# A summed weight factor made by an accumulating load instead of by VectorE, in all twelve blocks of seven products of a decoder trunk

## The chip, the cores and the metric

The kernel runs on one core of a Trainium2 chip. The metric is the device time of one execution in microseconds. The kernel before takes 912.77 us, the median of three runs from 911.77 to 912.87 us.

## What is computed

A trunk of two layers over 256 tokens of width 1024 in float32. Each layer is a gated feed-forward, a mixer with three groups of heads, and a second gated feed-forward, each between two RMS norms:

```python
def _swiglu(h, wg, wu, wd):
    return (jax.nn.silu(h @ wg) * (h @ wu)) @ wd

for l in range(DEPTH):                                       # DEPTH = 2
    f = _swiglu(_rmsnorm(h, ff1_norm_pre[l]), ff1_w_gate[l], ff1_w_up[l], ff1_w_down[l])
    h = h + 0.5 * _rmsnorm(f, ff1_norm_post[l])
    m = _hybrid_mixer(_rmsnorm(h, mix_norm_pre[l]), ...)     # SSD, pooling, attention; not touched here
    h = h + _rmsnorm(m, mix_norm_post[l])
    f = _swiglu(_rmsnorm(h, ff2_norm_pre[l]), ff2_w_gate[l], ff2_w_up[l], ff2_w_down[l])
    h = h + 0.5 * _rmsnorm(f, ff2_norm_post[l])
```

The gate and up weights are 1024 x 2816, the down weights 2816 x 1024. There are four feed-forwards, so four times the stage that the change touches.

## The kernel before

**Units and splits.** All weights come through one object, `Weights` (L50 to L158). A *unit* is a piece of 1 MB, 128 partitions x 2048 float32, loaded by SP into one of five `raw` buffers (`load`, L85). A *job* splits a unit for the matmuls: ScalarE writes a rounded copy `hi` (L114) and VectorE the rest, `lo = raw - hi` (L115), in two halves of 1024 columns (a "`hi` half", a "`lo` half"), into one of five pairs of buffers. A matmul product then is three passes: x_hi w_hi, x_hi w_lo, x_lo w_hi. A job may first make a sum of two units: VectorE adds them into the first one's buffer, at L113 half by half, or at L133 all at once ahead of the split. A job may end with an accumulating load: POOL issues a DMA that adds a unit from memory onto a buffer (`then`, L119). A job's `free` list names the `raw` buffers that it gives back.

**Feed-forward.** The 2816 hidden columns are eleven groups of 256. Groups 0 and 1 (FIRST) and the single ones 4, 7 and 10 (PAIRS) are plain products. Groups 2-3, 5-6 and 8-9 (QUADS, starting at 2, 5 and 8) are the *blocks of seven*: gate and up for 512 columns would be eight products of a 128 x 512 half row block of x by a 512 x 512 weight quarter, and Winograd's form of Strassen's scheme makes them from seven. I call the blocks of a feed-forward the *opening*, the *middle* and the *closing* one: three in each of four feed-forwards, twelve in all.

The right factors of the seven products are made from four weight quarters, g1, u1, g2 and u2 (gate and up, each with the upper and the lower half of the rows). With their left factors, in the order of the products in `ffn_quad`: g1 with X11; the first sum T1 = g1 + u1 with S1; the second sum T2 = T1 + u2 with S2; T3 = u1 + u2 with S3; g2 with X12; the *fourth factor* T4 = T2 + g2 with X22; and u2 with S4. T1, T2 and T4 are all made in the buffer of g1, by VectorE. T3 is made in the buffer of u1 by an accumulating load of u2, issued by POOL behind the sum T1. In the code the order of loads and splits is the order of the calls of `W.unit` and `W.job` in `plan_ffn` (L422).

**The products and their sums.** In `ffn_quad` (L563) the product of T2 is joined to that of g1 (L586, L587). The product of T3 lies in a bank `pd`: VectorE adds a term to it (L598) and reads it (L599), and then the product of T4 accumulates on top of it in the same bank. ScalarE takes silu of the result (L619), VectorE multiplies (L620, L630), and the hidden columns go to the transposes (L533, or a DMA) and the down products (`mm_rows`, L412).

**What sets the order.** Each engine works through its queue in order. The queues are laid down by a scheduler at build time: it takes the code's order, `issue_after` and `keep_in_program_order`, and moves what it holds to be ready. What it has laid down does not change on the chip. Inside the kernel `pump` (L136) hands out loads and splits when buffers are free. In the closing block `sum_next` (L133) makes the sum of T4 right behind the product of T1, ahead of its split; in the opening block it makes that of T2.

Of the kernel before, what the change touches and what calls it, by code (L numbers as in the profile page):

```python
# [15 lines left out]
ALU = mybir.AluOpType  # L16
AX = mybir.AxisListType

P = 128
# [3 lines left out]
DEPTH = 2  # L23
# [7 lines left out]
UNIT = 2048  # L31
# [4 lines left out]

FIRST, QUADS, PAIRS = (0, 1), (2, 5, 8), (4, 7, 10)

# [11 lines left out]
class Weights:  # L50
# [75 lines left out]
    def sum_next(self):  # L126
        u, sum_of, _, pieces, _ = self.jobs[self.split]
        assert sum_of and self.ready()
        x, op, y = sum_of
        step = self.units[u][1] // pieces  # L130
        for c in range(0, self.units[u][1], step):
            s = slice(c, c + step)
            self.nc.vector.tensor_tensor(self.raw[u][:, s], self.raw[x][:, s], self.raw[y][:, s], op=op)  # L133
        self.summed = self.split
# [27 lines left out]
def hybrid_trunk_kernel(ctx: ExitStack, tc: tile.TileContext, a, out: bass.AP):  # L162
# [259 lines left out]
    def plan_ffn(l, n):  # L422


        p = {}

        def down(i):
            p["d", i] = W.plan(a[f"ff{n}_d"][l, i])

        def pair(i):  # L430
            for k in "gu":
                p[k, i] = W.plan(a[f"ff{n}_{k}"][l, PAIRS.index(i)])

        for i in range(2):
            for k in range(2):
                p["f", i, k] = W.plan(a[f"ff{n}_f"][l, 2 * i + k], pieces=4)
        before = list(FIRST)
        for i in range(2, NU):
            if i in PAIRS:
                pair(i)  # L440
                for b in before:
                    down(b)
                before = [i]
            elif i in QUADS:
                src = a[f"ff{n}_q"][l, QUADS.index(i)]
# [7 lines left out]
                if not late:  # L453
# [108 lines left out]

    def ffn_quad(i, p, left, turn, downs, by_dma, two, take=None):  # L563

# [29 lines left out]
        if not late:  # L594
            downs[0]()
# [4 lines left out]
        if late:  # L600
            pump_behind(m)
        elif swap:
            pump_behind(m, SPLIT_BUFS, 1)
        else:
            W.pump()
        product(pa, left["X12"], p["g2", i], False)
        h0 = buf()
# [34 lines left out]
    def ffn(l, n, p, gain, turned, left, next_left, before_next, last, later=None):  # L642

        acc = [None, None]
        hT = {}
        by_dma, start = True, later is not None

        def two(i):
            return i == QUADS[-1] or i == QUADS[1] or i == QUADS[0] and not start

# [24 lines left out]
        for i in range(2, NU):  # L675
            if i not in QUADS + PAIRS:
                continue
            order = (1, 0) if i in QUADS or i == PAIRS[0] and two(QUADS[0]) else (0, 1)
            if hf:
# [3 lines left out]
            def turn():  # L683
# [7 lines left out]
                by_tile(turn_tile, 1)  # L691
                take()
# [16 lines left out]
            else:  # L709
                hf = ffn_quad(i, p, left, turn, [lambda b=b: both(b) for b in before], by_dma,  # L710
                              two(i))
                before = [i, i + 1]
# [532 lines left out]
def _layout(inp):  # L1245
# [18 lines left out]

    def quads(g, u):


        q = []
        for i in QUADS:
            for h in range(2):  # L1270
                for w in (g, u):
                    x = w[:, h * 512 : (h + 1) * 512, i * 256 : i * 256 + 512]
                    q.append(x.reshape(DEPTH, 4, P, 512).transpose(0, 2, 1, 3).reshape(DEPTH, P, UNIT))
        return np.stack(q, axis=1).reshape(DEPTH, len(QUADS), 4, P, UNIT)

    for n in (1, 2):
        g, u = f[f"ff{n}_w_gate"], f[f"ff{n}_w_up"]
        d[f"ff{n}_f"] = np.concatenate([half(g[:, :, :512]), half(u[:, :, :512])], axis=1)
        d[f"ff{n}_g"] = cols(g)[:, PAIRS]
        d[f"ff{n}_u"] = cols(u)[:, PAIRS]  # L1280
        d[f"ff{n}_q"] = quads(g, u)
        d[f"ff{n}_d"] = rows(f[f"ff{n}_w_down"])
# [39 lines left out]
```

## Time and profile before

| | |
|---|---|
| median of three runs | 912.77 us (911.77 to 912.87) |
| profiled execution: its own time, from its first to its last instruction (the span) | 910.8 us |
| granted TensorE clock | 0.999 |
| TensorE matmul, weight load | 99%, 84% busy |
| VectorE, ScalarE, GpSimd | 88%, 73%, 3% busy |
| moved by DMA | 198.63 MB, 12.58 MB of it by POOL's queue |

For the profiled execution no other time is recorded than the span; the runs' times also hold what lies around it. In the rows of the profile, PE is TensorE's matmuls, PEld its weight loads, DVE VectorE, ACT ScalarE, POOL GpSimd, SP the engine that issues most DMAs. A row of the timeline gives start and duration in us, the engine, the line, the operation, output and inputs, and how many instructions it joins; brackets give the idle time ahead of it and what ended it. Rows overlap somewhat: two VectorE instructions of 1.21 us take 2.35 us together.

### The profile page before, as it was taken

What the parts mean: (1) busy time and instruction counts of PE and PEld (TensorE: products, weight loads), DVE (VectorE), ACT (ScalarE), POOL (GpSimd) and SP (SyncE); (2) the same over time, 40 slices, a digit from 0 to 9 for tenths busy, and PEclk for the clock granted to TensorE, in tenths of its full rate; (3) what the DMA queues carried; (4) which work ended last, traced back from release to release, by engine and by line L of the source; (5) the groups of instructions that cost most, each with busy time, mean ns of one, the idle gap of its engine ahead of it and who ended that gap; (6) DMA issues with size and microseconds to landing.
All of it is one profiled execution on the core that took longest, in us unless ns stands there. A gap on an engine that the chain in (4) does not pass through costs nothing.

```text
span 910.8 us, 12262 instructions
## 1 busy us (share of the span) xinstructions
PE 901.0 (99%) x4556; PEld 760.6 (84%) x4556; DVE 801.6 (88%) x1068; ACT 665.9 (73%) x1045; POOL 29.8 (3%) x49
## 2 busy tenths in 40 slices
PE   8999999999999999999999999999999999999997
PEld 5888888889988888888888888888998888888885
DVE  6999988789878999988899999988989699999983
ACT  7776776778858777776878768767797668768772
POOL 0000000000001000000000000000000110000000
PEclk9999999999999999999999999999999999999999
DMA  9677977765355587768755968695824256978641
GB/s 360 181 274 227 384 188 282 251 214 204 78 195 208 128 314 205 289 162 288 244 187 149 339 196 299 173 305 200 298 109 162 93 173 180 323 214 298 177 124 47
DMA packets 60880, 198.63 MB, mean 218 GB/s; under 512 B 35858, under 2 KB 36370, under 8 KB 38804
## 3 DMA queue, kind: packets, MB, share of 16 engines
q1 hardware_dynamic: 58948, 185.13, 58.5%
q0 software_dynamic: 1728, 12.58, 7.3%
q8 instruction: 36, 0.59, 0.2%
q14 instruction: 24, 0.20, 0.1%
q10 hardware_dynamic: 144, 0.13, 0.0%
HBM read 188.65 MB, written 1.05 MB: 208 GB/s over the span
## 4 chain that ended last, share of the span: by engine, by line
PE 92%; DVE 5%; issue 2%; DMA 1%; ACT 0%; POOLq 0%; SPq 0%; POOL 0%; DVEq 0%
PE acc L412 29%; PE wk L559 23%; PE wk L390 13%; PE wk L359 9%; PE wk L350 6%; PE wk L361 5%; DVE lo L115 3%; PE wk L377 1%; PE wk L301 1%; DMA raw<-in_ff_f 1%; PE wk L1084 1%; PE acc L827 0%; DVE raw L113 0%; PE acc L897 0%; PE acc L1032 0%
## 5 line engine op out<-in xcount | busy, mean ns | idle before, releaser
L115 DVE TENSOR_TENSOR lo<-raw,hi 128x1024 fp32r<-128x1024 f32 (+2 forms) x452 | 464.3, 1076 | 37.4 <-ACT hi L114 36.8
L114 ACT ACTIVATE hi<-raw 128x1024 fp32r<-128x1024 f32 (+2 forms) x452 | 398.7, 937 | 72.2 <-DVE raw L113 30.1
L412 PE MATMUL acc<-hi,t 128*128 128x512 f32 x832 | 214.7, 391 | 0.0
L412 PEld LDWEIGHTS acc<-hi,t 128*128 128x128 f32 x832 | 155.0, 188 | 31.4
L412 PE MATMUL acc<-lo,t 128*128 128x512 f32 x416 | 113.4, 390 | 0.0
L559 PE MATMUL wk<-hi,n 128*128 128x512 f32 x384 | 100.5, 390 | 0.0
L390 PE MATMUL wk<-hi,xT 128*128 128x512 f32 x384 | 98.9, 393 | 0.2
L359 PE MATMUL wk<-xT,hi 128*128 128x512 f32 x384 | 95.9, 392 | 0.0
L412 PEld LDWEIGHTS acc<-lo,t 128*128 128x128 f32 x416 | 77.9, 188 | 16.3
L390 PEld LDWEIGHTS wk<-hi,xT 128*128 128x128 f32 x384 | 71.0, 188 | 16.4 <-ACT hi L114 1.6
L559 PEld LDWEIGHTS wk<-hi,n 128*128 128x128 f32 x384 | 71.8, 188 | 14.8
L359 PEld LDWEIGHTS wk<-xT,hi 128*128 128x128 f32 x384 | 69.8, 189 | 13.0
L559 PE MATMUL wk<-hi,xT 128*128 128x512 f32 x288 | 77.6, 390 | 0.1
L113 DVE TENSOR_TENSOR raw<-raw,raw 128x1024 f32<-128x1024 f32 x56 | 67.2, 1215 | 0.0
L559 PEld LDWEIGHTS wk<-hi,xT 128*128 128x128 f32 x288 | 53.8, 188 | 11.3 <-DVE t L599 0.4
L361 PEld LDWEIGHTS wk<-xT,lo 128*128 128x128 f32 x384 | 52.4, 190 | 3.8
L361 PE MATMUL wk<-xT,lo 128*128 128x256 f32 x384 | 53.5, 282 | 0.0
L559 PE MATMUL wk<-lo,n 128*128 128x512 f32 x192 | 52.1, 390 | 0.0
L390 PE MATMUL wk<-lo,xT 128*128 128x512 f32 x192 | 52.0, 391 | 0.0
L510 ACT ACTIVATE t<-t 128x1024 uint16<-128x1024 uint16 x31 | 32.6, 1055 | 24.4 <-DVE t L630 16.2
L390 PEld LDWEIGHTS wk<-lo,xT 128*128 128x128 f32 x192 | 36.0, 188 | 8.3 <-DVE lo L115 0.8
L559 PEld LDWEIGHTS wk<-lo,n 128*128 128x128 f32 x192 | 36.0, 188 | 7.7 <-DVE lo L115 0.2
(184 smaller groups left out, 947.8 us busy)
## 6 DMA issues: line engine op xcount, KB each, us to landing
raw<-in_ff_q SPq DMA_DIRECT2D x48, 1024.0 KB, 6.4
raw<-in_ff_d SPq DMA_DIRECT2D x44, 1024.0 KB, 5.1
raw<-in_ff_f SPq DMA_DIRECT2D x16, 1024.0 KB, 7.1
raw<-in_ff_q POOLq DMA_DIRECT2D x12, 1024.0 KB, 8.0
raw<-in_ff_g SPq DMA_DIRECT2D x12, 1024.0 KB, 4.8
raw<-in_ff_u SPq DMA_DIRECT2D x12, 1024.0 KB, 4.8
raw<-in_w_in SPq DMA_DIRECT2D x10, 1024.0 KB, 5.3
raw<-in_w_kvz SPq DMA_DIRECT2D x8, 1024.0 KB, 6.1
```

The costliest lines, as they stand in the source:

```text
L113: nc.vector.tensor_tensor(raw[:, s], self.raw[x][:, s], self.raw[y][:, s], op=op)
L114: self.act = nc.scalar.activation(hi[:, s], raw[:, s], AF.Copy)
L115: nc.vector.tensor_tensor(lo[:, s], raw[:, s], hi[:, s].bitcast(F32), op=ALU.subtract)
L301: pre_turn.last = nc.tensor.transpose(ps[:, k * P : (k + 1) * P], xn[i][:, k * P : (k + 1) * P], ident)
L350: nc.tensor.matmul(ps, w[:, k, s], y[:, k, :], start=i == 0 and k == 0, stop=i == 2 and k == KD - 1)
L359: nc.tensor.matmul(ps, hi[:, k, s], both[:, :, k, :], start=k == 0, stop=k == KD - 1)
L361: mm_side.end = nc.tensor.matmul(ps[:, S:], lo[:, k, s], xT[0][:, k, :], start=False, stop=k == KD - 1, skip_group_check=True)
L377: nc.tensor.matmul(ps, x[:, k, s], w[:, k, :], start=i == 0 and k == 0, stop=i == 2 and k == KD - 1)
L390: m = nc.tensor.matmul(ps, y[:, k, :], w[:, k, :], start=h == 0 and n == 0, stop=h == 1 and n == len(parts) - 1)
L412: m = nc.tensor.matmul(acc[b], x[:, j, s], w[:, j, b * 512 : (b + 1) * 512], start=first and j == 0 and i == 0, stop=last and j == 1 and i ...
L510: part = send.last = nc.scalar.activation(halves.rearrange("p (a n) -> p a n", a=2), x[:, :].bitcast(U16).rearrange("p (n a) -> p a n", a= ...
L559: nc.tensor.matmul(ps, x[:, k, :], w[:, k, :], start=first and n == 0, stop=n == len(parts) - 1, skip_group_check=not first)
```

## The change

T4 is no longer a sum by VectorE. The job of T2 gets an accumulating load behind it, of g2 onto the buffer of g1, which then holds T2 and so becomes T4. The job of T4 only splits that buffer. g2 is still loaded a second time on its own, for its own product, and its buffer is now given back after its own split and no longer after T4's. The rest of the diff has no effect in this form: `shape` returns the same groups for every feed-forward, `close` is never true (ahead of a block there is always FIRST or a single group), the weights' tensors are named by layer, and `sum_next` returns where there is no sum to make.

```diff
+def shape(l, n):
+    return (2, 5, 8), (4, 7, 10)
+
+def last_sum_loaded(l, n):
+    return True
...
     def sum_next(self):
         u, sum_of, _, pieces, _ = self.jobs[self.split]
-        assert sum_of and self.ready()
+        if not sum_of or not self.ready() or self.summed == self.split:
+            return
...
                 p["T1", i] = W.job(g1, (g1, ALU.add, u1), then=(u1, src[3]))
-                p["T2", i] = W.job(g1, (g1, ALU.add, u2))
+                p["T2", i] = W.job(g1, (g1, ALU.add, u2), then=(g1, src[2]) if loaded else None)
...
                 p["T3", i] = W.job(u1, free=(u1,))
                 g2 = W.unit(src[2])
...
-                p["g2", i] = W.job(g2)
+                p["g2", i] = W.job(g2, free=(g2,) if loaded else ())
...
-                p["T4", i] = W.job(g1, (g1, ALU.add, g2), free=(g1, g2))
+                p["T4", i] = W.job(g1, free=(g1,)) if loaded else W.job(g1, (g1, ALU.add, g2), free=(g1, g2))
...
         if late:
             pump_behind(m, SPLIT_BUFS - 1)
+            W.sum_next()
```

The scheduler lays the queues down anew. TensorE, second feed-forward of layer 0, opening block: the fourth factor (`hi67`, `lo67`) and u2 (`hi68`, `lo68`), before:

```order
L559 MATMUL wk362_3050<-hi68_3151,n366_3070 128x512 x4
L559 MATMUL wk362_3050<-lo68_3152,n366_3070 128x512 x2
L559 MATMUL wk373_3159<-hi67_3111,xT_108 128x512 x4
L559 MATMUL wk373_3159<-lo67_3112,xT_108 128x512 x4
L559 MATMUL wk373_3159<-hi67_3111,xT_108 128x512 x4
L559 MATMUL wk362_3050<-lo68_3152,n366_3070 128x512 x2
L559 MATMUL wk362_3050<-hi68_3151,n367_3071 128x512 x4
```

and now (L575 is the line that was L559):

```order
L575 MATMUL wk373_3155<-hi67_3111,xT_108 128x512 x4
L575 MATMUL wk373_3155<-lo67_3112,xT_108 128x512 x4
L575 MATMUL wk373_3155<-hi67_3111,xT_108 128x512 x4
L575 MATMUL wk362_3048<-hi68_3147,n366_3068 128x512 x4
L575 MATMUL wk362_3048<-lo68_3148,n366_3068 128x512 x4
L575 MATMUL wk362_3048<-hi68_3147,n367_3069 128x512 x4
```

The fourth factor's product has moved ahead of all of u2's; it stood behind six of its matmuls. In the opening blocks of layer 1 it is the same, and in the first feed-forward it now stands behind two, before behind seven.

VectorE in the same place: `lo65` is g2, `lo66` a down unit, `lo69` the next gate unit; L587, L598 and L599 are the sums named above. Before:

```order
L115 TENSOR_TENSOR lo65_3083<-raw55_2843,hi65_3082 128x1024 x2
L115 TENSOR_TENSOR lo66_3089<-raw56_3018,hi66_3088 128x1024 x2
L587 TENSOR_TENSOR wk362_3050<-wk362_3050,t355_3033 128x512
L115 TENSOR_TENSOR lo67_3112<-raw51_2533,hi67_3111 128x1024
L113 TENSOR_TENSOR raw51_2533<-raw51_2533,raw55_2843 128x1024
L115 TENSOR_TENSOR lo68_3152<-raw53_2819,hi68_3151 128x1024 x2
L115 TENSOR_TENSOR lo67_3112<-raw51_2533,hi67_3111 128x1024
L598 TENSOR_TENSOR wk373_3159<-wk373_3159,t355_3033 128x512
L115 TENSOR_TENSOR lo69_3175<-raw57_3080,hi69_3174 128x1024
L599 TENSOR_TENSOR t363_3063<-t363_3063,wk373_3159 128x512
```

and now:

```order
L603 TENSOR_TENSOR wk362_3048<-wk362_3048,t355_3031 128x512
L126 TENSOR_TENSOR lo65_3081<-raw55_2840,hi65_3080 128x1024 x2
L126 TENSOR_TENSOR lo66_3089<-raw56_3016,hi66_3088 128x1024 x2
L126 TENSOR_TENSOR lo67_3112<-raw51_2530,hi67_3111 128x1024 x2
L126 TENSOR_TENSOR lo68_3148<-raw53_2816,hi68_3147 128x1024 x2
L615 TENSOR_TENSOR wk373_3155<-wk373_3155,t355_3031 128x512
L126 TENSOR_TENSOR lo69_3171<-raw57_3078,hi69_3170 128x1024
L616 TENSOR_TENSOR t363_3061<-t363_3061,wk373_3155 128x512
```

The sum (its other half stood ten rows higher) is gone, both halves of the fourth factor stand ahead of u2, and five `lo` halves stand between the first of them and L616, which was L599.

VectorE, same feed-forward, closing block: `lo88` is T3, `lo89` g2, `lo90` u2, `lo91` the fourth factor. Before:

```order
L115 TENSOR_TENSOR lo88_3797<-raw71_3563,hi88_3796 128x1024
L133 TENSOR_TENSOR raw70_3531<-raw70_3531,raw73_3649 128x1024
L115 TENSOR_TENSOR lo89_3829<-raw73_3649,hi89_3828 128x1024 x2
L133 TENSOR_TENSOR raw70_3531<-raw70_3531,raw73_3649 128x1024
L115 TENSOR_TENSOR lo90_3865<-raw72_3586,hi90_3864 128x1024 x2
L586 TENSOR_TENSOR t419_3847<-wk422_3874,t419_3847 128x512
L587 TENSOR_TENSOR wk420_3849<-wk420_3849,t419_3847 128x512
L115 TENSOR_TENSOR lo91_3890<-raw70_3531,hi91_3889 128x1024 x2
L598 TENSOR_TENSOR wk423_3899<-wk423_3899,t419_3847 128x512
L599 TENSOR_TENSOR t421_3862<-t421_3862,wk423_3899 128x512
```

and now:

```order
L126 TENSOR_TENSOR lo88_3793<-raw71_3558,hi88_3792 128x1024
L126 TENSOR_TENSOR lo89_3825<-raw73_3644,hi89_3824 128x1024 x2
L126 TENSOR_TENSOR lo90_3863<-raw72_3581,hi90_3862 128x1024 x2
L602 TENSOR_TENSOR t419_3845<-wk422_3870,t419_3845 128x512
L603 TENSOR_TENSOR wk420_3847<-wk420_3847,t419_3845 128x512
L126 TENSOR_TENSOR lo91_3886<-raw70_3526,hi91_3885 128x1024 x2
L615 TENSOR_TENSOR wk423_3893<-wk423_3893,t419_3845 128x512
L616 TENSOR_TENSOR t421_3860<-t421_3860,wk423_3893 128x512
```

Only the sums have gone; TensorE's queue is the same there. SP's queue holds the same transfers in the same order throughout.

More of the change, by code (lines that the diff above doesn't have):

```diff
@@ L35 @@
 TAIL = 4
-FIRST, QUADS, PAIRS = (0, 1), (2, 5, 8), (4, 7, 10)
+FIRST = (0, 1)
+def shape(l, n):
+    return (2, 5, 8), (4, 7, 10)
+def last_sum_loaded(l, n):
+    return True
 C_ID, C_U, C_SGT, C_NEG, C_CNT, C_CS = 0, 128, 256, 384, 512, 1024
@@ L425, in plan_ffn @@
         p = {}
+        QUADS, PAIRS = shape(l, n)
+        loaded = last_sum_loaded(l, n)
         def down(i):
@@ L431, in pair @@
             for k in "gu":
-                p[k, i] = W.plan(a[f"ff{n}_{k}"][l, PAIRS.index(i)])
+                p[k, i] = W.plan(a[f"ff{l}{n}_{k}"][PAIRS.index(i)])
         for i in range(2):
@@ L444, in plan_ffn @@
             elif i in QUADS:
-                src = a[f"ff{n}_q"][l, QUADS.index(i)]
+                src = a[f"ff{l}{n}_q"][QUADS.index(i)]
                 g1, u1, u2 = (W.unit(src[k]) for k in (0, 1, 3))
@@ L452, in plan_ffn @@
                 late, swap = i == QUADS[-1], i != QUADS[0]
-                if not late:
+                close = before[0] in QUADS
+                if not late and not close:
                     down(before[0])
@@ L456, in plan_ffn @@
                 g2 = W.unit(src[2])
-                p["g2", i] = W.job(g2)
+                if not late and close:
+                    down(before[0])
+                p["g2", i] = W.job(g2, free=(g2,) if loaded else ())
                 for b in before[1:]:
@@ L561, in product, with ffn_quad @@
         W.done(job)
-    def ffn_quad(i, p, left, turn, downs, by_dma, two, take=None):
+    def ffn_quad(i, p, left, turn, downs, by_dma, two, QUADS, close, loaded):
         late, swap = i == QUADS[-1], i != QUADS[0]
@@ L593, in ffn_quad @@
             W.pump()
-        if not late:
+        if not late and not close:
             downs[0]()
@@ L605, in ffn_quad @@
             W.pump()
+        if not late and close:
+            downs[0]()
         product(pa, left["X12"], p["g2", i], False)
@@ L646, in ffn @@
         by_dma, start = True, later is not None
+        QUADS, PAIRS = shape(l, n)
         def two(i):
-            return i == QUADS[-1] or i == QUADS[1] or i == QUADS[0] and not start
+            return i in QUADS and (i != QUADS[0] or not start)
         hf = [ffn_first(0, p, later is not None, turned, by_dma=by_dma)]
@@ L677, in ffn @@
                 continue
-            order = (1, 0) if i in QUADS or i == PAIRS[0] and two(QUADS[0]) else (0, 1)
+            order = (1, 0) if i in QUADS or before[0] == QUADS[0] and two(QUADS[0]) else (0, 1)
             if hf:
@@ L690, in turn @@
                     return
-                by_tile(turn_tile, 1)
+                by_tile(receive if two(before[0]) else turn_tile, 1)
                 take()
@@ L710, in ffn @@
                 hf = ffn_quad(i, p, left, turn, [lambda b=b: both(b) for b in before], by_dma,
-                              two(i))
+                              two(i), QUADS, before[0] in QUADS, last_sum_loaded(l, n))
                 before = [i, i + 1]
@@ L1263, in half, with quads @@
         return x.reshape(DEPTH, 2, 4, P, 512).transpose(0, 1, 3, 2, 4).reshape(DEPTH, 2, P, UNIT)
-    def quads(g, u):
+    def quads(g, u, starts):
         q = []
-        for i in QUADS:
+        for i in starts:
             for h in range(2):
                 for w in (g, u):
-                    x = w[:, h * 512 : (h + 1) * 512, i * 256 : i * 256 + 512]
-                    q.append(x.reshape(DEPTH, 4, P, 512).transpose(0, 2, 1, 3).reshape(DEPTH, P, UNIT))
-        return np.stack(q, axis=1).reshape(DEPTH, len(QUADS), 4, P, UNIT)
+                    x = w[h * 512 : (h + 1) * 512, i * 256 : i * 256 + 512]
+                    q.append(x.reshape(4, P, 512).transpose(1, 0, 2).reshape(P, UNIT))
+        return np.stack(q).reshape(len(starts), 4, P, UNIT)
     for n in (1, 2):
@@ L1278, in _layout @@
         d[f"ff{n}_f"] = np.concatenate([half(g[:, :, :512]), half(u[:, :, :512])], axis=1)
-        d[f"ff{n}_g"] = cols(g)[:, PAIRS]
-        d[f"ff{n}_u"] = cols(u)[:, PAIRS]
-        d[f"ff{n}_q"] = quads(g, u)
+        for l in range(DEPTH):
+            starts, singles = shape(l, n)
+            d[f"ff{l}{n}_g"] = cols(g[l : l + 1])[0, list(singles)]
+            d[f"ff{l}{n}_u"] = cols(u[l : l + 1])[0, list(singles)]
+            d[f"ff{l}{n}_q"] = quads(g[l], u[l], starts)
         d[f"ff{n}_d"] = rows(f[f"ff{n}_w_down"])
```

## The prediction

> **What bounds the kernel now.** I read the engines' shares first, then the chain that ended last, then TensorE's own waits, because an engine can be busy and still be the one that waits. The page of the profile:
>
> ```profile
> span 910.8 us, 12262 instructions
> PE 901.0 (99%) x4556; PEld 760.6 (84%) x4556; DVE 801.6 (88%) x1068; ACT 665.9 (73%) x1045; POOL 29.8 (3%) x49
> PE 92%; DVE 5%; issue 2%; DMA 1%; ACT 0%; POOLq 0%; SPq 0%; POOL 0%; DVEq 0%
> ```
>
> TensorE is busy for all but 9.8 us of the span, and 92% of the chain is its own. A busy TensorE need not be at full pace, so I look at the spacing in the chain in order of time, and at all that TensorE and its weight load waited for (us in total, times, longest):
>
> ```profile
> 78.45 10.91 PE acc L412 x48
> 102.95 10.88 PE wk L559 x48
> ...
> PE acc L225 <- DVE zeros L214: 2.3, 1, 2.3
> PE wk L533 <- DVE t L630: 0.7, 1, 0.7
> PE wk L301 <- DVE n L291: 0.2, 1, 0.2
> ...
> PEld wk L559 <- DVE t L599: 0.4, 1, 0.4
> ```
>
> 48 matmuls take 10.91 us in the one and 10.88 us in the other, 0.227 us each: the pace does not change between a down product (L412) and a product of a block of seven (L559). In the whole program TensorE waits three times for another engine, and of the three only the 0.7 us behind L630 lies in a feed-forward stage; the 0.4 us behind L599 is the weight load's. So VectorE, 88% busy, is hidden everywhere but at one place: the opening block of the first feed-forward. That place, in the chain, then on TensorE, then on VectorE:
>
> ```profile
> 53.79 2.27 DVE raw L113 x2
> 72.23 0.63 PE wk L533 x4
> ...
> 59.91 1.07 PE L559 MATMUL wk<-hi,n 128*128 128x512 f32 x4
> 61.85 1.19 PE L559 MATMUL wk<-hi,xT 128*128 128x512 f32 x4
> 72.23 0.63 PE L533 MATMUL wk<-ident,t 128*128 128x128 f32 x4 [0.67 <-DVE t L630]
> ...
> 53.71 2.35 DVE L113 TENSOR_TENSOR raw<-raw,raw 128x1024 f32<-128x1024 f32 x2
> 61.12 0.68 DVE L599 TENSOR_TENSOR t<-t,wk 128x512 f32<-128x512 f32 x1
> ```
>
> The two L113 rows at 53.71 are the sum of the fourth factor, the very work that goes. They stand on the chain, but the chain only says that VectorE's queue from there on released TensorE at 72.23, 0.67 us late. That 0.67 us, not the 2.27 us, is what their removal can pay.
>
> **What goes.** The fourth factor's sum is two instructions in each of twelve blocks: 16 on L113 and 8 on L133 (in the closing blocks `sum_next` makes it).
>
> ```profile
> L113 DVE TENSOR_TENSOR raw<-raw,raw x56: 1208/1215/1221, 28.9 to 847.1; 128x1024 f32<-128x1024 f32 x56
> L133 DVE TENSOR_TENSOR raw<-raw,raw x16: 1210/1216/1221, 34.7 to 857.9; 128x1024 f32<-128x1024 f32 x16
> ```
>
> 24 x 1.215 = 29.2 us of VectorE. In eleven blocks TensorE never waited behind them, so there they are worth nothing; what hides them is the 0.227 us pace above. In the first block VectorE's queue comes 2.27 us earlier to L630, more than the 0.67 us it was late, so that wait is gone: -0.67. The 0.4 us behind L599 stays. TensorE now reaches the fourth product after two matmuls of the u2 product (59.91 + 2 x 0.227 = 60.36), not after seven (61.85). VectorE, from 53.79 with nothing idle, does five `lo` halves of 1.14 (half of 2.27, as in the row), L598 and L599 (1.3): 53.79 + 5.7 + 1.3 = 60.8. A wait of 0.4 us before, of 0.5 after: 0.1 lost.
>
> **What comes.** Twelve more accumulating loads of 1 MB on POOL's queue, each with a wait for the second sum's split. POOL has only other such loads and the norms' powers behind it, and is busy 3% of the span, so the instruction itself costs nothing. No load of SP is moved past another; g2's buffer no longer waits for the sum, so the load that takes it starts up to 2 us sooner. The price is latency: the fourth factor is now there when the load has landed. The rows of the twelve accumulating loads of before, one landing alone, one behind other loads, and SP's two loads issued ahead of the latter:
>
> ```profile
> L119 POOL DMA_DIRECT2D raw<-in_ff_q x12: 853/868/1035, 31.9 to 842.0; - x12
> DMA to landing us min/median/max: 7.8/8.0/11.3
> ...
> DMA to landing us min/median/max: 7.9/7.9/7.9
> ...
> DMA to landing us min/median/max: 11.2/11.2/11.2
> ...
> 519.70 0.53 SPq L85 DMA_DIRECT2D raw<-in_ff_d  x1
> 520.33 0.39 SPq L85 DMA_DIRECT2D raw<-in_ff_q  x1
> ```
>
> The 7.9 is the one issued at 396.50, with no load of SP about; the 11.2 is that of 523.0. How long may one take before TensorE feels it? In a closing block (second feed-forward of layer 0), on VectorE, ScalarE, TensorE and SP, with the two rows by which I time POOL's start behind VectorE:
>
> ```profile
> 405.57 3.50 DVE L115 TENSOR_TENSOR lo<-raw,hi 128x1024 fp32r<-128x1024 f32 x3 [1.55 <-ACT hi L114]
> 417.19 2.35 DVE L115 TENSOR_TENSOR lo<-raw,hi 128x1024 fp32r<-128x1024 f32 x2
> 420.18 0.69 DVE L599 TENSOR_TENSOR t<-t,wk 128x512 f32<-128x512 f32 x1
> ...
> 413.11 2.00 ACT L114 ACTIVATE hi<-raw 128x1024 fp32r<-128x1024 f32 x2
> ...
> 423.30 1.07 PE L559 MATMUL wk<-hi,xT 128*128 128x512 f32 x4
> ...
> 409.09 0.33 SPq L85 DMA_DIRECT2D raw<-in_ff_g  x1
> ...
> 303.64 1.22 DVE L113 TENSOR_TENSOR raw<-raw,raw 128x1024 f32<-128x1024 f32 x1
> 305.16 0.89 POOL L119 DMA_DIRECT2D raw<-in_ff_q  x1 [11.67 <-DVE raw L113]
> ```
>
> The second sum's split ends with the second of the three `lo` rows at 405.57, at 407.9. POOL starts 0.3 us behind VectorE (304.86 to 305.16). From the landing on: 1.05 us for the first `hi` half on ScalarE (two, overlapping, take 2.00), two `lo` halves (2.3), then L598 and L599, 1.3 from the end of the `lo` at 419.54 to 420.87. L599 reads the bank into which the fourth product accumulates, and it stands on VectorE behind the `lo` halves, so TensorE, due at 423.30, waits for all of it: 4.7 us with 0.05 for the semaphore. The landing may take 423.3 - 407.9 - 0.3 - 4.7 = 10.4 us; I carry 10.3. Past that, each us of landing costs TensorE one us. In the opening blocks of the three later feed-forwards, in a middle block, and in the first of all:
>
> ```profile
> 311.65 2.35 DVE L115 TENSOR_TENSOR lo<-raw,hi 128x1024 fp32r<-128x1024 f32 x2
> ...
> 332.95 1.07 PE L559 MATMUL wk<-hi,n 128*128 128x512 f32 x4
> ...
> 312.90 0.33 SPq L85 DMA_DIRECT2D raw<-in_ff_d  x1
> ...
> 84.96 4.62 DVE L115 TENSOR_TENSOR lo<-raw,hi 128x1024 fp32r<-128x1024 f32 x4
> ...
> 110.95 1.07 PE L559 MATMUL wk<-hi,xT 128*128 128x512 f32 x4
> ...
> 38.15 4.62 DVE L115 TENSOR_TENSOR lo<-raw,hi 128x1024 fp32r<-128x1024 f32 x4
> ```
>
> Opening: the split ends at 314.00, and the fourth product is now due at 332.95, where the u2 product stood. Behind the landing are 1.05, five `lo` halves (5.7), L598 and L599, 8.1 us together: 18.95 - 0.3 - 8.1 = 10.5 us of room. Middle: from 89.6 at the latest to 110.95 are 21.4 us, and 0.3 + 11.3 + 4.7 go in with 5 to spare. First of all: the split ends with the third of four rows, at 41.6, and VectorE comes to the fourth factor at 53.79, so 53.79 - 41.6 - 0.3 - 1.1 = 10.8 us.
>
> So the unknown is the landing, from 7.9 (alone) to 11.2 (two loads ahead). In the closing block one load, at 409.09, is issued 0.9 us behind POOL's start (408.2); in the opening one, at 312.90, 1.4 us ahead of it (314.3). Neither is the case of 523.0, where two whole loads went first. How much one load can add follows from the DMA engines' shares while one moves alone, first in 8.1 us with an accumulating load, then in 3.6 us with a plain one:
>
> ```profile
> q0 software_dynamic: 144, 1.05, 68.5%
> ...
> q1 hardware_dynamic: 143, 1.05, 80.5%
> ```
>
> That is 5.5 us of all sixteen engines for an accumulating load and 2.9 us for a plain one. If all of the plain one goes first or in between, the landing is 7.9 + 2.9 = 10.8 us, 0.5 too late in a closing block; if none, 7.9. The opening block's load has 1.4 us of start, so about half of it is left: 9.4, and 1.1 us to spare. For the closing blocks I take the end nearest to 7.9, since the load is issued later and the row of 523.0, with loads ahead, is the wrong way round. Then nothing is late.
>
> [...] No run here shows an accumulating load with a plain one right behind it.
>
> **The sum.** 910.8 - 0.67 + 0.1 = 910.2 for a span like that of the profile. The median of the runs shown, 912.77, lies 1.97 above the span; what is launched and ended around it doesn't change. Predicted: 912.2 us.
>
> **The rivals.** *Landing late* (slower). The loads land in 11.2 us, as at 523.0, in each block with little room: 4 closing blocks x 0.9, 3 opening x 0.7, the first of all 0.4, together 6.1, and 918.3 us. For it: SP's next load but one comes sooner than before, and all use the same engines. Against: in the row of 11.2 the other loads were issued 3.3 and 2.7 us ahead. It decides from 10.73 us on average, where 4 x 0.43 + 3 x 0.23 - 0.57 reaches 1.83 us. *The gap only moves* (no change). The first block's load lands just past its 10.8 us beside SP's loads, VectorE, in order, stands idle at the fourth factor, and L630 is as late as before; or the closing blocks lose 0.15 us each. Either gives back the 0.6: 912.8. For it: the rows at 59.91 and 61.85 show TensorE there without slack. Against: 10.8 us of room is 2.9 more than a load takes alone. *VectorE's chain is worth its length* (faster). Taken at its word, the chain loses 2.27 us, and 910.5 comes out. For it: the rows stand on the chain. Against: TensorE has no gap of that size there; 0.7 + 0.4 is all.
>
> **How the numbers follow.** The forecast has 0.62, the moved gap 0.22, late landing 0.11, the chain's length 0.05. About 0.2% (1.83 us) is what a measurement of this kernel can tell from no change; the three runs of before span 1.1 us. The forecast and the moved gap are inside it, late landing outside on the slow side, the chain's length just outside on the fast side: faster 0.05, same 0.84, slower 0.11. The range reaches down to 911.0 (the forecast less the spread of the runs, rounded down) and up to 915.0 (a landing of 10.8 us, a whole load in front, in the closing blocks, with 0.8 more for the opening ones), and leaves out most of late landing and the chain's length.
>
> **What would show it.** Right: VectorE's busy time is 29 us less, the page's `ff_q` loads on POOL are 24, TensorE's wait behind the row of L630 is gone, and TensorE's list of waits has no new row of the fourth product. Landing late would show as waits of ScalarE's L114 for POOL's loads in the closing blocks of more than 4 us, with TensorE idle at the fourth product behind L599. The moved gap would show as TensorE still waiting 0.5 us or more near 72 us. The forecast is wrong if the landings there are above 10.7 us, or if TensorE's pace of 0.227 us changes.

## The result and the profile after

The changed kernel takes 922.37 us (median of four runs, 920.58 to 924.0) where the kernel before takes 912.68 (911.77 to 912.87): 1.0109 times as long, 95% interval 1.0093 to 1.0125. Forecast were 912.2 us and a range up to 915.0. The profiled execution took 921.25 us, with a span of 919.5 against 910.8.

The page's engine shares and chain:

```profile
span 919.5 us, 12295 instructions
PE 905.0 (98%) x4556; PEld 761.3 (83%) x4556; DVE 776.8 (84%) x1044; ACT 664.2 (72%) x1045; POOL 40.2 (4%) x61
...
PE 62%; DVE 11%; DMA 11%; ACT 9%; issue 6%; SPq 0%; POOLq 0%; DVEq 0%; POOL 0%; ACTq 0%
```

VectorE does 24 instructions and 24.8 us less, and TensorE does the same 4556 matmuls. But the chain, 92% TensorE before, is now 62% TensorE, and transfers hold 11% of it for 1%. TensorE's waits and those of its weight load (us in total, times, longest):

```profile
PE wk L575 <- ACT hi L125: 2.8, 1, 2.8
PE wk L575 <- DVE t L616: 2.0, 1, 2.0
PE acc L424 <- ACT t L262: 0.5, 1, 0.5
...
PEld acc L424 <- ACT t L262: 2.5, 6, 0.7
```

The 0.7 us wait behind L630 (now L649) is gone, as forecast. In its place stand a wait of 2.0 us in the first opening block (L575 is the line of all seven products, L616 the step with which VectorE reads the bank that the fourth product accumulates in), one of 2.8 us for a `hi` half, and six short ones of the down products (L424) for the received hidden columns (L262). Both long ones are at a *fourth product*: as in the prediction, that is the product of the fourth factor. How late the same matmul starts in the two traces (its lag), at places along the program:

| first matmul of | before, us | after, us | late by |
|---|---|---|---|
| first feed-forward, middle block | 89.19 | 90.61 | 1.42 |
| first feed-forward, fourth product of the closing block | 152.04 | 156.51 | 4.47 |
| mixer of layer 0, product with B | 206.59 | 212.39 | 5.80 |
| second feed-forward of layer 0 | 285.19 | 290.97 | 5.78 |
| first feed-forward of layer 1 | 459.87 | 466.42 | 6.55 |
| second feed-forward of layer 1 | 730.63 | 737.99 | 7.36 |
| a down product near its end | 890.82 | 899.35 | 8.53 |

So 5.8 of the 8.7 us are lost in the first feed-forward, and 0.8, 0.8 and 1.2 in the other three. Three places show how.

**The opening block of the first feed-forward.** ScalarE and VectorE, TensorE's fourth product, then the two loads of that moment (issue, and us from issue to landing):

```profile
52.60 7.70 ACT L125 ACTIVATE hi<-raw 128x1024 fp32r<-128x1024 f32 x8 [4.16 <-DMA raw<-in_ff_d]
...
53.69 6.90 DVE L126 TENSOR_TENSOR lo<-raw,hi 128x1024 fp32r<-128x1024 f32 x6 [2.17 <-ACT hi L125]
62.24 0.68 DVE L616 TENSOR_TENSOR t<-t,wk 128x512 f32<-128x512 f32 x1
...
62.98 1.20 PE L575 MATMUL wk<-hi,xT 128*128 128x512 f32 x4 [2.04 <-DVE t L616]
...
41.95 0.88 POOL L130 DMA_DIRECT2D raw<-in_ff_q  x1 [9.01 <-DVE lo L126]
...
42.84 0.33 SPq L96 DMA_DIRECT2D raw<-in_ff_d  x1
...
raw<-in_ff_q POOLq DMA_DIRECT2D x1, 1024.0 KB, 9.7
raw<-in_ff_d SPq DMA_DIRECT2D x1, 1024.0 KB, 9.7
```

It is not the new load that anyone waits for first, but the down unit that SP issues 0.9 us behind it: it takes 9.7 us, where before it took 4.8. ScalarE stands 4.16 us, VectorE 2.17, as much as the sum that was removed. L616 starts at 62.24, where L599 started at 61.12. TensorE comes to the fourth product with two matmuls of the u2 product ahead of it and no longer seven, and stands from 60.9 to 62.98. (Two of the expectations below put this wait at the u2 product.)

**The middle block of the first feed-forward, and what it does to the closing one.** VectorE near 108 us, SP and the landing of its row, then ScalarE and TensorE in the closing block, and a window of 4 us there (busy time and instructions of TensorE, its weight loads, VectorE, ScalarE and POOL, then the granted clock, the DMA engines' share and GB/s):

```profile
108.38 0.17 DVE L825 COPY s<-row 128x8 f32<-128x8 f32 x1 [4.60 <-DMA row<-in_row]
...
96.84 0.45 SPq L781 DMA_DIRECT2D row<-in_row  x1
...
row<-in_row SPq DMA_DIRECT2D x1, 268.0 KB, 11.5
...
151.58 5.80 ACT L125 ACTIVATE hi<-raw 128x1024 fp32r<-128x1024 f32 x6 [5.69 <-DMA raw<-in_ff_q]
...
156.51 1.17 PE L575 MATMUL wk<-hi,xT 128*128 128x512 f32 x4 [2.81 <-ACT hi L125]
...
158.00:162.00 4.00, 4.00 (x12) 3.17 (x11) 3.51 (x4) 0.46 (x1) 0.00 (x0) 0.57 0.95 356
```

and before, the same COPY, which is the mixer's copy of its decay row, written far down in the code:

```profile
107.58 0.16 DVE L805 COPY s<-row 128x8 f32<-128x8 f32 x1
...
95.43 0.49 SPq L761 DMA_DIRECT2D row<-in_row  x1
...
row<-in_row SPq DMA_DIRECT2D x1, 268.0 KB, 8.2
```

The scheduler had laid this COPY between L598 and L599 (now L615 and L616), where its row had long landed (95.43 + 8.2 = 103.6). It now stands ahead of L615 and of the split before that, and the sum ahead of it is gone: VectorE comes to it at 103.8 and, in order, waits 4.60 us for a row that was issued 1.4 us later and takes 11.5 us. The splits behind it are late, buffers come free late, the closing block's second sum is split late (POOL issues the load behind it at 141.93; in copy_behind, where the COPY is held back, at 139.92), and its fourth factor lands at 151.6, with TensorE due at 153.7. TensorE stands 2.81 us, and the twelve matmuls from 157.52 to 161.85 take 0.36 us each instead of 0.227, at a granted clock of 0.57 in the window from 158 to 162.

**A closing block elsewhere** (second feed-forward of layer 0), VectorE, ScalarE and TensorE after, and one row of ScalarE before:

```profile
424.60 2.36 DVE L126 TENSOR_TENSOR lo<-raw,hi 128x1024 fp32r<-128x1024 f32 x2 [1.98 <-ACT hi L125]
428.20 4.62 DVE L126 TENSOR_TENSOR lo<-raw,hi 128x1024 fp32r<-128x1024 f32 x4
432.75 0.68 DVE L649 TENSOR_TENSOR t<-wk,t 128x512 f32<-128x512 f32 x1
...
423.50 5.80 ACT L125 ACTIVATE hi<-raw 128x1024 fp32r<-128x1024 f32 x6 [4.51 <-DMA raw<-in_ff_q]
433.46 1.06 ACT L526 ACTIVATE t<-t 128x1024 uint16<-128x1024 uint16 x1 [3.68 <-DVE t L649]
...
429.08 1.07 PE L575 MATMUL wk<-hi,xT 128*128 128x512 f32 x4
```

```profile
426.04 1.06 ACT L510 ACTIVATE t<-t 128x1024 uint16<-128x1024 uint16 x1 [4.67 <-DVE t L630]
```

The fourth product itself starts on time: 429.08, against 423.30 before, exactly the 5.78 us of lag that the program already has. But ScalarE starts its `hi` halves 10.4 us later than before (413.11), so 4.6 us more than that lag. Behind that split, in the same two queues, stand the splits of the down unit and of the next gate unit, then L649, then the sending of the hidden columns: 433.46 against 426.04, 1.6 us more than the lag. The down products wait for those columns.

### The profile page after: what moved, and what is told of

Its sections match the earlier page's. It is cut to its first block, busy times and chain, and to the rows that moved or that the text cites. A ratio compares the mean times of both kernels' runs of the same rounds, so it can differ in the third digit from the quotient of the medians.

```text
span 919.5 us, 12295 instructions
## 1 busy us (share of the span) xinstructions
PE 905.0 (98%) x4556; PEld 761.3 (83%) x4556; DVE 776.8 (84%) x1044; ACT 664.2 (72%) x1045; POOL 40.2 (4%) x61
## 4 chain that ended last, share of the span: by engine, by line
PE 62%; DVE 11%; DMA 11%; ACT 9%; issue 6%; SPq 0%; POOLq 0%; DVEq 0%; POOL 0%; ACTq 0%
PE acc L424 21%; PE wk L402 13%; PE wk L575 10%; DVE lo L126 7%; DMA raw<-in_ff_q 7%; PE wk L362 6%; ACT hi L125 6%; PE wk L371 4%; PE wk L373 2%; PE wk L389 1%; DMA row<-in_row 1%; DVE raw L124 1%; ACT t L538 1%; DMA raw<-in_ff_d 1%; DMA raw<-in_ff_g 1%
## 5 line engine op out<-in xcount | busy, mean ns | idle before, releaser
L424 PE MATMUL acc<-hi,t 128*128 128x512 f32 x832 | 216.6, 392 | 0.7 <-ACT t L262 0.5
L424 PEld LDWEIGHTS acc<-hi,t 128*128 128x128 f32 x832 | 154.8, 188 | 34.1 <-ACT t L262 2.5
L424 PE MATMUL acc<-lo,t 128*128 128x512 f32 x416 | 113.8, 390 | 0.1
L575 PE MATMUL wk<-hi,n 128*128 128x512 f32 x384 | 100.7, 390 | 0.0
L424 PEld LDWEIGHTS acc<-lo,t 128*128 128x128 f32 x416 | 77.9, 188 | 16.9 <-DVE lo L126 0.5
L575 PEld LDWEIGHTS wk<-hi,n 128*128 128x128 f32 x384 | 71.8, 188 | 14.8
L575 PE MATMUL wk<-hi,xT 128*128 128x512 f32 x288 | 78.2, 394 | 4.9 <-ACT hi L125 2.8
L575 PEld LDWEIGHTS wk<-hi,xT 128*128 128x128 f32 x288 | 54.3, 190 | 17.5 <-ACT hi L125 3.6
L575 PE MATMUL wk<-lo,n 128*128 128x512 f32 x192 | 51.4, 389 | 0.0
L124 DVE TENSOR_TENSOR raw<-raw,raw 128x1024 f32<-128x1024 f32 x40 | 48.1, 1216 | 0.0
L362 PE MATMUL wk<-xT,hi 128*128 128x256 f32 x320 | 42.5, 284 | 0.0
```

The costliest lines, as they stand in the source:

```text
L124: nc.vector.tensor_tensor(raw[:, s], self.raw[x][:, s], self.raw[y][:, s], op=op)
L362: nc.tensor.matmul(ps, w[:, k, s], y[:, k, :], start=i == 0 and k == 0, stop=i == 2 and k == KD - 1)
L424: m = nc.tensor.matmul(acc[b], x[:, j, s], w[:, j, b * 512 : (b + 1) * 512], start=first and j == 0 and i == 0, stop=last and j == 1 and i ...
L575: nc.tensor.matmul(ps, x[:, k, :], w[:, k, :], start=first and n == 0, stop=n == len(parts) - 1, skip_group_check=not first)
```

## The experiments

Times are medians; each is compared with the kernel before on the same chip (912.5 us beside the first four, then 911.91, 912.28 and 912.5), with the ratio and its 95% interval.

### Which blocks, and the moved COPY

Here `last_sum_loaded` is asked for each block (i is 2 in an opening, 5 in a middle, 8 in a closing block).

```diff
-        loaded = last_sum_loaded(l, n)
+                loaded = i == 8
```

> The accumulating load in the four closing blocks alone, VectorE's sum in the other eight. Theory A (the fourth product itself is fed just in time, but ScalarE and VectorE reach everything behind it 1.5 to 2.3 us late, so that the downs wait for the received hidden columns: 0.8 to 1.2 us per feed-forward): 915.7 to 917.2 us, with the wait of TensorE's weight load at L424 for L262 in all four feed-forwards. Theory B (only the fourth factor's landing counts, and it is in time, as predicted): 912.7 us. Theory C (the landing in the first feed-forward's closing block is late by itself, by 3 us): 919 to 921 us.

917.48 us, 1.0057 (1.0042 to 1.0072): half of the whole loss, and theory A, 0.3 us above its range. TensorE's only wait at a fourth product is 0.6 us, in the last closing block, where the load took 10.6 us; its weight load waits for the columns eight times.

```profile
PE wk L575 <- ACT hi L125: 0.6, 1, 0.6
...
PEld acc L424 <- ACT t L262: 4.3, 8, 0.7
```

With `i == 2`:

> The accumulating load in the four opening blocks alone, VectorE's sum in the other eight. Theory A (in the first feed-forward the load holds back the down unit issued 0.9 us behind it by 4.3 us, which gives back on VectorE all of the sum's 2.3 us and costs TensorE a 2 us wait in place of the 0.7 us one; the three later openings cost nothing): 913.8 to 914.6 us. Theory B (the wait behind L630 goes and nothing comes in its place, as predicted): 912.0 us.

913.96 us, 1.0019 (1.0009 to 1.0028): theory A. In its trace the down unit again takes 9.7 us, and all of the loss lies in the first feed-forward's block: the same matmul is 0.2 us early ahead of the fourth product there, 2.4 us late behind the block, and 2.4 us late to the end.

With `i == 5`, and the COPY held back:

> The accumulating load in the four middle blocks alone, VectorE's sum in the other eight, and the COPY held back as in the run before. Theory A (in a middle block the load is hidden, TensorE waits nowhere for it, the loads behind it have slack): 912.3 to 913.2 us, the same as before. Theory B (every accumulating load costs TensorE by holding back the plain loads beside it, some 0.8 us each): 915 to 916 us. If VectorE's 2.4 us per block were worth anything: under 911.5 us.

913.47 us, 1.0007 (0.9998 to 1.0017), not told from before. In its trace every matmul behind the start of the first feed-forward keeps its distance to the same matmul of before to within 0.15 us. Theory A, though 0.3 us above its range: nothing lost, and nothing won.

The changed kernel with the COPY alone held back:

```diff
-        nc.vector.scalar_tensor_tensor(e, x16, -1.0, x16, op0=ALU.mult, op1=ALU.min)
-        nc.vector.tensor_copy(negA, row[:, R_AL : R_AL + HEADS])
+        m = nc.vector.scalar_tensor_tensor(e, x16, -1.0, x16, op0=ALU.mult, op1=ALU.min)
+        with tc.issue_after(m.ins):
+            nc.vector.tensor_copy(negA, row[:, R_AL : R_AL + HEADS])
```

> The changed kernel, with the 128x8 COPY of the mixer's params row held back behind the instruction that it stands next to in the code, so that it no longer stands among the splits of the first feed-forward's middle block. Theory A (the COPY waits 4.60 us there for its row, that makes the closing block's second sum late, and TensorE then stands 2.97 us before the fourth product and runs at half pace for some 1.7 us more): 917.5 to 918.5 us, and no stall above 0.5 us at that product. Theory B (the accumulating load of that block, which lands 9.6 us after issue, is late by itself): 921 to 922.5 us and the 2.97 us wait stays.

920.58 us, 1.0089 (1.0074 to 1.0104). Neither theory: between the medians 1.8 us came back, not 4. That alone is not clear of noise, for the two kernels were measured apart and their runs overlap (919.78 to 921.78 and 920.58 to 924.0). The traces are clearer: the wait has gone from 2.81 us to

```profile
PE wk L575 <- ACT hi L125: 0.8, 1, 0.8
```

and no window there shows a lower clock (1.00 in each of three from 150 to 160). Why not 4? In the middle block VectorE still waits, now for ScalarE, which waits for the kernel's constants:

```profile
106.58 2.36 DVE L126 TENSOR_TENSOR lo<-raw,hi 128x1024 fp32r<-128x1024 f32 x2 [2.63 <-ACT hi L125]
...
104.88 0.31 ACT L247 ACTIVATE after_r<-cst 128x128 fp32r<-128x128 f32 x1 [2.71 <-DMA cst<-in_consts]
```

The load of these constants (544 KB) is issued 4.5 us behind the middle block's accumulating load and lands 10.0 us after its issue; before, with no such load ahead, it took 5.8 us, and ScalarE waited 1.75 us for it. So the COPY's 4.60 us hid a second wait: without it L615 starts at 108.86 instead of 110.74, 1.9 us earlier. By itself this wait costs nothing that shows: middle_only has it too (2.59 us), at 913.47 us, not told from before.

Added up, in medians: closing 5.0, opening 1.5, COPY 1.8 make 8.3 of 9.7 us; the rest is within what the intervals leave open, or comes from the blocks together: TensorE waits 0.8 us for the fourth factor in the first feed-forward's closing block here, and starts that product on time in closing_only (151.85, before 152.04).

### Closing blocks: the queue or the transfer

Two runs each try one of the two explanations. First, the split of the down unit (d) that stands behind the fourth product's goes ahead of it:

```diff
+                if late:
+                    down(before[0])
                 p["T4", i] = W.job(g1, free=(g1,)) if loaded else W.job(g1, (g1, ALU.add, g2), free=(g1, g2))
-                if late:
-                    down(before[0])
```

> closing_only (917.5 us) with one thing moved: in the closing blocks the split of the down unit d stands ahead of the fourth product's split on ScalarE and VectorE; the loads are issued as before it, TensorE's order is the same. Theory A (ScalarE's and VectorE's queues stand some 4.8 us for the accumulating load, with d's and g's splits behind it ready to go, and that is what makes everything later 1.9 us late): d's 2.3 us of VectorE go into the wait, 912.7 to 914.2 us. Theory B (the plain loads of the next units land late because the accumulating load takes the DMA engines): 916.5 to 917.5 us.

911.9 us, 0.9999 (0.999 to 1.0009): all 5.0 us are back, 0.8 us below theory A's range. ScalarE in the block shown above, what is left of the wait, and the landing of the gate unit issued 0.9 us behind the accumulating load:

```profile
412.40 2.00 ACT L125 ACTIVATE hi<-raw 128x1024 fp32r<-128x1024 f32 x2
417.01 3.90 ACT L125 ACTIVATE hi<-raw 128x1024 fp32r<-128x1024 f32 x4 [2.62 <-DMA raw<-in_ff_q]
...
raw<-in_ff_g SPq DMA_DIRECT2D x1, 1024.0 KB, 9.6
```

d's two halves at 412.40 now use time in which the queue stood, and the hidden columns are sent at 424.89. The loads are as slow as in closing_only: the accumulating one takes 9.5 us in both, the gate unit 9.6 and the up unit 9.8 (before 4.7 and 4.8). The move alone, in the kernel before:

> The kernel before (VectorE makes all twelve sums), with only the split of d ahead of the fourth product's in the closing blocks. If that move only uses time in which the queues stand for the accumulating load, it is worth nothing here: 911.6 to 912.4 us. If it is worth something by itself (under 911.2 us), part of what d_split_first won back was not the load's cost; if it harms (over 913 us), the load's cost was larger than the pair showed.

912.57 us, 1.0003 (0.9995 to 1.0012): worth nothing where no load is waited for. Second, the transfer without the wait: VectorE makes the sums, and an accumulating load that nobody needs runs beside.

```diff
+            m = nc.gpsimd.tensor_copy(self.mark, lo[:, cols - 1 : cols].bitcast(F32))
+            with self.tc.issue_after(m.ins):
+                nc.gpsimd.dma_start(self.spare[:, :UNIT], then[0], accum_op=ALU.add)
```

> The kernel before (VectorE makes all twelve sums), with one more accumulating load of 1 MB in each closing block, from POOL as the second sum's split ends, into a tensor in memory that nobody reads. Theory A (ScalarE's and VectorE's wait in the queue is the cost of the closing blocks): 912.3 to 913.4 us. Theory B (the load's share of the DMA engines is): 915 to 917.5 us.

912.22 us, 1.0 (0.9991 to 1.001). By itself this run shows less than it was made for. POOL, SP and the gate unit:

```profile
408.44 0.85 POOL L132 DMA_DIRECT2D spare<-in_ff_q  x1
...
408.48 0.33 SPq L96 DMA_DIRECT2D raw<-in_ff_g  x1
...
raw<-in_ff_g SPq DMA_DIRECT2D x1, 1024.0 KB, 4.8
```

POOL's copy ahead of the load made it 0.9 us later than in the change, the two issues fell together, and the gate unit was not held up here; only the up unit was, with 7.6 us. That the slow loads cost nothing in the closing blocks is shown by d_split_first, where both units land as late as in the change and no time is lost. So what costs the 5.0 us is standing in two in-order queues.

### The opening block: which of two loads goes first

The same idle load, in the opening blocks:

> The kernel before, with the same idle accumulating load in the four opening blocks alone. Theory A (in the first feed-forward's opening block the load holds back the down unit issued 0.9 us behind it, whatever its own landing is for): that unit's hi half starts near 52 us, not 48.3, and with VectorE's sum still to do behind it TensorE loses 1.4 to 4 us: 914.0 to 916.5 us, nothing in the three later feed-forwards. Theory B (the new place of the fourth factor's split on VectorE costs it, not the transfer): 912.5 us.

914.15 us, 1.0023 (1.0014 to 1.0033): here the transfer alone costs no less than the change does. Yet the profiled execution, the fastest of ten at 912.49, shows none of it; the nine others took 913.48 to 915.02, and where they lose it is not traced. POOL, SP and ScalarE:

```profile
41.73 0.86 POOL L132 DMA_DIRECT2D spare<-in_ff_q  x1
...
41.81 0.34 SPq L96 DMA_DIRECT2D raw<-in_ff_d  x1
...
43.52 5.78 ACT L125 ACTIVATE hi<-raw 128x1024 fp32r<-128x1024 f32 x6
```

POOL's one-column copy ahead of it had put the load 0.8 us later, the two issues fell together, SP's ended 0.44 us ahead of POOL's (42.15 and 42.59), and ScalarE ran through, with no wait for the down unit. That pointed to the order of the two loads. A first attempt to make the accumulating load second, with the same copy behind the third product's first half:

> opening_only (914.0 us) with one thing changed, in the first feed-forward's opening block alone: POOL issues the accumulating load not as the second sum's split ends but as the first half of the third product's split does (a one-column copy of that half on POOL ahead of it), some 6 us later, so that the down unit's load goes first. Theory A (the accumulating load held that unit back): its hi half starts at 48.3 to 49 us, not 52, the wait for L616 at the u2 product goes, and so does the 0.7 us wait behind the opening's last DVE step: 911.0 to 912.2 us. Theory B (a later load is only a later fourth factor): 914 to 916 us.

926.18 us, 1.0151 (1.0138 to 1.0165). Neither theory was tested, because the copy did not do what it was for. POOL, VectorE and ScalarE:

```profile
48.03 5.65 POOL L130 COPY mark<-lo 128x1 f32<-128x1 f32 x1 [15.23 <-DVE lo L126]
53.63 0.87 POOL L132 DMA_DIRECT2D raw<-in_ff_q  x1
...
46.75 6.89 DVE L126 TENSOR_TENSOR lo<-raw,hi 128x1024 fp32r<-128x1024 f32 x6
...
65.90 5.79 ACT L125 ACTIVATE hi<-raw 128x1024 fp32r<-128x1024 f32 x6 [15.71 <-DMA raw<-in_ff_q]
```

The copy of 128 elements took 5.65 us and ended 0.04 us behind VectorE's six splits; the load went out at 53.6, with plain ones ahead and beside it (SP's issues at 49.13, 51.40 and 53.67), and landed at 65.9. TensorE stood 12.4 us. The run with all mends and this copy lost the same:

> The changed kernel, all twelve fourth factors by load, with the three mends together: COPY held back, d's split ahead of the fourth product's in the closing blocks, the load of the first opening block issued later. If the three causes are all there is: 910.8 to 912.2 us, at or up to 1 us below the kernel before. If they act on each other (loads that start later in one block make the next block late): 913 to 916 us.

927.25 us, 1.016 (1.0146 to 1.0174). With the first opening block left to VectorE instead:

> The changed kernel with the COPY held back and d's split ahead in the closing blocks, and the sum of the first feed-forward's opening block alone left to VectorE (eleven loads). If the three causes are all there is: 911.7 to 912.9 us, as before. If the middle blocks' loads make the first closing block late even so: 913 to 914.5 us.

913.45 us, 1.0005 (0.9996 to 1.0014): eleven loads, not told from before by the interval. But the median lies in the range that I gave to a late first closing block, and the runs spread from 911.56 to 914.56. In the profiled execution, the slowest of them, 1.8 us are lost between the middle block of the first feed-forward and the mixer, with a wait of 0.67 us at 170.18 for received hidden columns.

The delay again, now without POOL's compute, by two tiny stores ahead of the load on POOL's queue:

```diff
+                for c in range(2 if len(then) == 3 else 0):
+                    m = nc.gpsimd.dma_start(self.mark[:, c : c + 1], lo[:, cols - 1 : cols].bitcast(F32))
+                    order.enter_context(self.tc.issue_after(m.ins))
                 nc.gpsimd.dma_start(self.raw[then[0]][:, :UNIT], then[1], accum_op=ALU.add)
```

> opening_only (914.0 us) with two DMAs of one column each, from the second sum's split to memory that nobody reads, issued by POOL ahead of the accumulating load in the first feed-forward's opening block: at 0.87 us for an issue that puts the load some 1.7 us later, behind the down unit's issue 0.9 us after the split, and asks nothing of POOL's compute. Theory A (which of the two loads goes first decides): the down unit's hi half starts near 48.3 us, not 52, no wait for L616 at the u2 product, and the 0.7 us wait behind the opening's last VectorE step goes: 911.0 to 912.3 us. Theory B (any accumulating load in flight there costs the same): 913.5 us or more.

912.5 us, 1.0001 (0.9992 to 1.001): the loss is gone, so the order decides, as theory A has it; the gain that I expected beside it is not there. POOL's load, SP's, the down unit's landing, ScalarE and TensorE:

```profile
43.09 0.95 POOL L134 DMA_DIRECT2D raw<-in_ff_q  x1
...
42.85 0.34 SPq L96 DMA_DIRECT2D raw<-in_ff_d  x1
...
raw<-in_ff_d SPq DMA_DIRECT2D x1, 1024.0 KB, 5.6
...
53.63 5.80 ACT L125 ACTIVATE hi<-raw 128x1024 fp32r<-128x1024 f32 x6 [3.10 <-DMA raw<-in_ff_q]
...
61.74 1.19 PE L581 MATMUL wk<-hi,xT 128*128 128x512 f32 x4 [1.16 <-DVE t L622]
```

Issued 0.24 us behind the down unit's load, and not 0.89 us ahead of it, the accumulating load leaves it 5.6 us instead of 9.7. Now the accumulating load is second and lands at 53.6, so a wait of 1.16 us at the fourth product takes the place of the two of before, 0.67 and 0.4 us.

### All twelve together, and the price of accumulating

> All twelve fourth factors by load, with the COPY held back, d's split ahead of the fourth product's in the closing blocks, and in the first opening block the two one-column DMAs ahead of the accumulating load. If the order of two loads, the moved COPY and the two in-order queues are the whole loss: 910.8 to 912.6 us, at or up to 1.3 us below the kernel before. If the blocks act on each other: 913 to 916 us.

912.36 us, 1.0002 (0.9993 to 1.001). With the COPY, the split's place and the order of two loads put right, the loss is gone from the median and from the trace, and all twelve loads are worth nothing against VectorE's sums. Eight of the twelve runs lie at 911.6 to 912.6 us, the traced one among them, and four at 913.9 to 914.6; what costs these four some 2 us is not traced. Last, the changed kernel with the COPY held back and the fourth factor's load a plain one:

> copy_behind (920.6 us) with the load of the fourth factor not accumulating in all twelve blocks: it overwrites the sum, so the fourth product uses a wrong factor; the same bytes, the same wait behind the second sum's split, the same issue from POOL. Theory A (what the accumulation costs the 16 DMA engines, 5.5 us of them for 2.9, makes the landing and the loads beside it late): 913.0 to 914.8 us, landing in 5.5 to 7 us. Theory B (any load behind the second sum's split is too late there): 918 to 920.6 us.

910.61 us, 0.9988 (0.9978 to 0.9997): 9 to 10 us less than copy_behind, the same kernel with accumulation, 1.3 below before, and below the range that I had given to theory A. Nine of the twelve plain loads land 5.0 to 5.2 us after their issue, where the accumulating ones took 9.5 to 10.5. What TensorE still waits for lies ahead of the feed-forwards' products:

```profile
PE acc L240 <- DVE zeros L229: 2.3, 1, 2.3
PE wk L316 <- DVE n L306: 0.2, 1, 0.2
```

That is what removing the sum would pay if its replacement were a plain load. It is no version of the kernel, since it leaves the fourth factor's sum out.

## Why the prediction was wrong

**What goes** was right. VectorE's removed work was worth the 0.67 us wait and little more: the wait behind L630 is gone in every kernel with the first opening block's load, and the run with plain loads, where the replacement is nearly free, gains 1.3 us. In middle blocks the sums were worth nothing (middle_only, 913.47 us).

**The landing** was mis-sized, but that was not what failed. I took 7.9 us for closing blocks; there the new loads landed in 9.6, 9.6, 9.6 and 10.4, and all twelve in 9.5 to 10.5. The 7.9 is the landing of a load issued alone, and no trace shows it for the fourth factor in a closing block: with SP's gate unit issued 0.9 us behind POOL's load (414.70 and 413.84), the landing was 9.6, so 1.7 us more with a plain load behind than alone. Even so it was below the room of 10.3 in three of the four closing blocks, and the fourth product was on time, or nearly, except in the first feed-forward.

**The step that failed** is the one that made room the only measure: "Past that, each us of landing costs TensorE one us", and by silence nothing before that. The room was measured for the product that needs the load. What stands behind its split in ScalarE's and VectorE's queues was not: the down unit, the next gate unit, L630 and the sending of hidden columns. With the fourth product on time, the sending came 1.6 us late, and TensorE waited for the columns. closing_only and d_split_first show it: 5.0 us, of which TensorE stood 0.6 at a fourth product, where a load of 10.6 us went past the room.

**"No load of SP is moved past another"** was true and beside the point. The accumulating load is issued 0.89 us ahead of a plain one of another queue, and the prediction counted only the other direction (2.9 us for a plain load in front). The plain load behind it lost 4.9 us in the first opening block (9.7 instead of 4.8). opening_only and opening_load_behind show it: 1.5 us. I had computed that block's room as 10.8 us, and the load took 9.7: inside the room, and the block still lost, because of the other load. The term "a wait of 0.4 us before, of 0.5 after" had VectorE at work from 53.79 on with nothing idle; it stood 2.17 us just before, and the wait was 2.04.

**The moved COPY** I did not see at all. The order of the instructions showed it, in a place of which no term spoke. copy_behind puts it at 1.8 us between medians, where I expected 4: I had counted the whole 4.60 us of VectorE as the COPY's, and 2.63 us of waiting for ScalarE's constants stood behind it.

**The rivals.** *Landing late* (918.3) had the nearest time and the wrong mechanism: landings were 9.8 us on average, below the 10.73 from which it was to decide, and where ready work stood ahead of the wait, in d_split_first, they cost nothing (911.9 us). *The gap only moves* describes opening_load_behind, not the change. Of the signs that I named, three held (VectorE's busy time, 24.8 us less instead of 29; 24 loads; no wait behind L630); "no new row of the fourth product" failed, and so did the one that I gave to *Landing late*: ScalarE waits of more than 4 us for POOL's loads are there, with TensorE mostly not idle at the fourth product. And "above 10.7 us", named as what would prove the forecast wrong, never came: it was wrong with every landing below that.

What stays open is the last 1.4 us of the sum of the parts, the four longer runs of all_twelve_behind, and how often the two loads of the first opening block change places in a kernel in which their issues lie within 0.1 us.

## What to carry to other kernels

When a wait is moved from an instruction to a transfer, everything queued behind the instruction that waits can be late with it, on each engine whose queue stands (here the sending of the hidden columns came 1.6 us late, with the fourth product on time): measure how much lateness the last of them can bear, not only the product that needs the data, and put ready work ahead of the wait (5.0 us here: closing_only takes 1.0057 times the time of before, d_split_first 0.9999). A slow transfer also has to be costed against the plain loads issued just behind it (the down unit took 9.7 us instead of 4.8). And after any edit under a scheduler, look through the new order for an instruction that waits for a transfer and has moved ahead of busy work, wherever it belongs in the code (the COPY, 4.60 us).

## What the runs showed that was not expected

**A one-column copy on POOL stood 5.65 us** beside VectorE's splits and ended with the last of them; in idle_load_closing the same copy took 1.11 us at 407.39, and VectorE's run of three splits ended at 408.46, 0.04 us ahead of it. In opening_load_later it started at 48.03, behind the first of the six splits, and ended with the last of them, five splits of 1.15 us later; in all_twelve_mended it took 5.65 us again, from 47.92. What held it is not shown.

```profile
407.39 1.11 POOL L130 COPY mark<-lo 128x1 f32<-128x1 f32 x1 [10.56 <-DVE lo L126]
...
404.96 3.50 DVE L126 TENSOR_TENSOR lo<-raw,hi 128x1024 fp32r<-128x1024 f32 x3 [1.47 <-ACT hi L125]
```

**Behind two short waits of TensorE its clock fell as well.** Behind the 2.81 us wait of the changed kernel the granted clock was 0.57 of full over 4 us; in opening_only, behind a wait of 2.05 us, 0.50 over 3 us:

```profile
64.00:67.00 3.00, 3.00 (x9) 2.35 (x8) 3.00 (x4) 0.25 (x1) 0.00 (x0) 0.50 0.97 366
```

Nine matmuls lie in those 3 us, and fifteen in the next 3. The changed kernel's own wait of 2.0 us at the same place was followed by full pace (a granted clock of 1.00 in each window from 60 to 70 us), so the length of the wait alone does not tell.
